# Storing the bias table of the sliding attention: one transfer in the second chunk of the projections, or sixteen in the seventh

## The chip, the cores and the metric

The kernel runs on one core of one Trainium2 chip. The metric is the device time of one execution in microseconds (us), as the median of the runs. The engines are named as in the profile: PE (TensorE, with PEld for its weight loads), DVE (VectorE), ACT (ScalarE), POOL (GpSimd) and SP (SyncE, which in this kernel issues nearly all DMAs). Each engine executes its instructions in the order in which they stand, and waits on semaphores for what others make.

## The reference, cut to what matters

The reference chains two transformer blocks over 2048 positions of width 1024. The first has a projection of 4096 columns, a differential and a dilated attention; the second is a sliding-window attention with sinks and a learned bias by distance.

```python
def first_block(x, p, mix_norm_g, w_in, ...):
    h = rms_norm(x, mix_norm_g[i])
    u = h @ w_in[i]                                   # (2048, 1024) @ (1024, 4096)
    dq, dk, dv, bq, bk, bv, z = jnp.split(u, IN_SPLIT_IDX, axis=-1)
    ...
    y = jnp.concatenate([a, b], axis=-1) * jax.nn.silu(z)

def banded_attention(q, k, v, t5_table, window, sinks=None):   # second block, window 128, 16 heads
    ...
    dist = nprev * Q_BLOCK + jnp.arange(Q_BLOCK)[:, None] - jnp.arange(kc)[None, :]
    valid = (dist >= 0) & (dist < window) & (kpos >= 0)
    bias = jnp.take(t5_table, t5_bucket(dist), axis=0)
    s = jnp.where(valid, s + bias[None, :, :, None], NEG)
    p = jax.nn.softmax(jnp.concatenate([s, sk], axis=-1), axis=-1)[..., :-1]
```

The bias of a head depends only on the distance between query and key. For 128 queries by 256 keys it is therefore a band matrix, every row of which is the row above, shifted by one.

## The kernel before, in words

The stages run one after the other: `phase_a` (the projection of the first block), `phase_b1` and `phase_b2` (its two attentions), `phase_c` (its output), `phase_d` (the sliding attention) and `phase_e` (the last product). A scheduler lays out the instructions of each engine while the program is built, by its own estimate of times and by the free buffers of the pools.

**phase_a** takes the 4096 columns in eight chunks of 512, in the order dv, bv, dk, dq, bk, bq, z0, z1 (`order`). A chunk is 16 tiles of 128 rows. A tile is 24 matmuls into one of four PSUM buffers `psm` (lines 190 to 192): eight pieces k of the depth, each with three products, since both operands are split in a high and a low part. After its last matmul a tile is evacuated by ACT and DVE into buffers of the pool `a_e` (14 buffers, printed as `t` or `t2`) and from there stored to DRAM: `evac_v` (lines 110 to 113, stores `s_dv` and `s_bv`), `norm_qk` and `trans_qk` (lines 128 to 161, stores such as `s_bq`), `evac_z` (lines 119 to 123, store `s_sz`).

The weights of the next chunk are loaded by `load_w` (lines 98 to 101): a DMA on SP into `wraw` (three buffers), a copy on ACT into the high part of `w`, a subtraction on POOL into the low part (ten buffers `w`). The ACT copies of the weights stand in the same queue as the evacuations of the tiles. With ten buffers `w`, two of the eight pieces of the next chunk can be converted while a chunk runs and three more wait in `wraw`; the other three are loaded as the chunk ends.

All these DMAs are issued by SP, in its order. The program gives them eight completion semaphores in turn, and a DMA waits for the one before it on its semaphore; so SP has at most eight DMAs open and stands still when the oldest of them isn't done.

**The bias table.** `prep_swa` is called (as `extra`) after the first chunk. One matmul (line 976) makes the 128 bias values of the 16 heads, DVE writes them into the middle of `e_vec`, 16 partitions (one for each head) of 384 numbers with -1e30 at both sides, and line 978 stores this row 128 times for every head into the DRAM table `s_toep` (16 x 128 x 384 numbers, 3,145,728 bytes):

```python
nc.sync.dma_start(scr["toep"], vec.unsqueeze(1).broadcast_to([16, P, 384]))
```

`phase_d` reads the table back with a row step of 383 instead of 384 numbers, which gives the shifted rows (`e_bias`, line 1092, first issued at 2159.2 us).

Of the kernel before, what the change touches and what calls it, by code (L numbers as in the profile page):

```python
# [7 lines left out]
F32 = mybir.dt.float32  # L8
# [8 lines left out]
P = 128  # L17
# [24 lines left out]
def phase_a(tc, c, x, w_in, mix_g, qk_gains, scr, extra):  # L42
    nc = tc.nc
    with (
# [19 lines left out]
        def tmp(dt=F32):  # L64
            return ep.tile([P, 512], dt, name="t2", tag="t2")
# [3 lines left out]
        def load_x(g, f):  # L69
            for j in range(4):  # L70
                t = tmp()
                nc.sync.dma_start(t, x[0, (4 * g + j) * P:(4 * g + j + 1) * P, 512 * f:512 * f + 512])
                xs[g, f, j] = t

        def trans_x(g, k):
            ps = pt.tile([P, 512], F32, name="pst")
            for j in range(4):
                nc.tensor.transpose(ps[:, j * P:(j + 1) * P], xs[g, k // 4, j][:, (k % 4) * P:(k % 4 + 1) * P], c["id"])
            nc.scalar.activation(hh[g][:, k], ps, AF.Copy, scale=g_t[:, k:k + 1])
            nc.vector.scalar_tensor_tensor(hl[g][:, k], ps, g_t[:, k:k + 1], hh[g][:, k].bitcast(F32),  # L80
                                           ALU.mult, ALU.subtract)
# [3 lines left out]
        def square_x(g, f):  # L85
            if f == 0:
                sq2s[g] = sp.tile([P, 2, 4], F32, name="sq2")
            for j in range(4):
                nc.scalar.activation(tmp(), xs.pop((g, f, j)), AF.Square, accum_out=sq2s[g][:, f, j:j + 1])
            if f == 1:  # L90
                ssq = sp.tile([P, 4], F32, name="ssq")
                nc.vector.tensor_add(ssq, sq2s[g][:, 0], sq2s[g][:, 1])
                rsqrt_dve(nc, sp, ssq, D, rstd[:, 4 * g:4 * g + 4])
                nc.vector.tensor_scalar(half_rstd[:, 4 * g:4 * g + 4], rstd[:, 4 * g:4 * g + 4], 0.5, None, ALU.mult)

        def load_w(ch, k):
            raw = wrp.tile([P, 512], F32, name="wraw")
            nc.sync.dma_start(raw, w_in[0, k * P:(k + 1) * P, ch * 512:(ch + 1) * 512])
            w = wp.tile([P, 2, 512], F32R, name="w")
            nc.scalar.activation(w[:, 0], raw, AF.Copy)  # L100
            nc.gpsimd.tensor_sub(w[:, 1], raw, w[:, 0].bitcast(F32))  # L101
            return w

        def evac_v(nm, t, ps):
            rs = rstd[:, t:t + 1]
            rows = slice(t * P, (t + 1) * P)
            w_ = 128 if nm == "dv" else 64
            ev = [tmp(F32R).rearrange("p (n w) -> p n w", w=w_) for _ in range(2)]
            psv = ps.rearrange("p (n w) -> p n w", w=w_)
            nc.scalar.activation(ev[0], psv, AF.Copy, scale=rs)  # L110
            nc.vector.scalar_tensor_tensor(ev[1], psv, rs, ev[0].bitcast(F32), ALU.mult, ALU.subtract)  # L111
            for i in range(2):
                nc.sync.dma_start(scr[nm][rows][:, :, i], ev[i].bitcast(F32))

        def evac_z(nm, t, ps):
            hr = half_rstd[:, t:t + 1]
            col = 512 * (nm == "z1")
            th = tmp()
            nc.scalar.activation(th, ps, AF.Tanh, scale=hr)
            nc.vector.tensor_scalar(th, th, 1.0, hr, ALU.add, ALU.mult)  # L120
            sz = tmp()
            nc.vector.tensor_tensor(sz, ps, th, ALU.mult)
            nc.sync.dma_start(scr["sz"][t * P:(t + 1) * P, col:col + 512], sz)
# [16 lines left out]
        def trans_qk(nm, t, qn):  # L140
            gain = gq[{"dq": 0, "dk": 1, "bq": 2, "bk": 3}[nm]]
            pq = pt.tile([P, 512], F32, name="pst")
            for f in range(4):
                nc.tensor.transpose(pq[:, f * P:(f + 1) * P], qn[:, f * P:(f + 1) * P], c["id"])
            th = tmp(F32R).rearrange("p (f t) -> p f t", f=4)
            tl = tmp(F32R).rearrange("p (f t) -> p f t", f=4)
            if nm == "bk":
                src, dh, dl = [w.rearrange("p (b u g) -> p g b u", u=16, g=4) if w is pq else
                               w.rearrange("p f (a g u) -> p g (f a) u", a=2, g=4) for w in (pq, th, tl)]
                nc.scalar.activation(dh.rearrange("p g b u -> p b u g"), src.rearrange("p g b u -> p b u g"),  # L150
                                     AF.Copy, scale=gain)
                for g in range(4):
                    nc.vector.scalar_tensor_tensor(dl[:, g], src[:, g], gain, dh[:, g].bitcast(F32),
                                                   ALU.mult, ALU.subtract)
            else:
                pq3 = pq.rearrange("p (f t) -> p f t", f=4)
                nc.scalar.activation(th, pq3, AF.Copy, scale=gain)
                nc.vector.scalar_tensor_tensor(tl, pq3, gain, th.bitcast(F32), ALU.mult, ALU.subtract)
            for i, src in ((0, th), (1, tl)):
                for e in range(2):  # L160
                    nc.sync.dma_start(scr[nm][:, e, i].rearrange("f d t -> d f t")[:, :, t * P:(t + 1) * P],
                                      src[64 * e:64 * e + 64].bitcast(F32))
# [13 lines left out]
        for i, ap in enumerate(qk_gains):  # L176
            t = cp.tile([P, 1], F32, name=f"qk_gain{i}")
            for half in range(2):
                nc.sync.dma_start(t[64 * half:64 * half + 64], ap.rearrange("o d -> d o"))
            gq.append(t)  # L180
        pend = []
        for oi, (nm, ch) in enumerate(order):
            nxt = []
            for t in range(NT):
                g, j = divmod(t, 4)
                ps = pm.tile([P, 512], F32, name="psm")
                for k in range(KD):
                    ah = hh[g][:, k, j * P:(j + 1) * P]
                    al = hl[g][:, k, j * P:(j + 1) * P]
                    nc.tensor.matmul(ps, ah, cur[k][:, 0], start=k == 0, stop=False)  # L190
                    nc.tensor.matmul(ps, al, cur[k][:, 0], start=False, stop=False)  # L191
                    nc.tensor.matmul(ps, ah, cur[k][:, 1], start=False, stop=k == KD - 1)  # L192
                if oi == 0 and g < 3:
                    if j == 0:
                        load_x(g + 1, 0)
                        load_x(g + 1, 1)
                    trans_x(g + 1, 2 * j)
                    trans_x(g + 1, 2 * j + 1)
                    if j == 3:
                        for f in range(2):  # L200
                            square_x(g + 1, f)
                if t >= 8 and oi + 1 < len(order):
                    nxt.append(load_w(order[oi + 1][1], t - 8))
                if len(pend) > 1 or pend and nm == "z0":
                    trans_qk(*pend.pop(0))
                if nm in ("dv", "bv"):
                    evac_v(nm, t, ps)
                elif nm in ("z0", "z1"):
                    evac_z(nm, t, ps)
                else:  # L210
                    pend.append((nm, t, norm_qk(nm, t, ps)))
            if oi == 0:
                extra(pt)
            cur = nxt
# [745 lines left out]
def prep_swa(tc, c, scr, table, onehot, sinks, pm):  # L960


    nc = tc.nc
    sk8 = c["const"].tile([P, 16], F32, name="e_sk")
    nc.sync.dma_start(sk8, sinks.broadcast_to([P, 16]))
    nc.vector.tensor_scalar(sk8, sk8, 8.0, None, ALU.mult)
    c["sk8"] = sk8
    with tc.tile_pool(name="p_c", bufs=1) as cp:
        tb = cp.tile([32, 16], F32, name="e_tb")
        nc.sync.dma_start(tb, table)  # L970
        oh = cp.tile([32, P], F32, name="e_oh")
        nc.sync.dma_start(oh, onehot)
        vec = cp.tile([16, 384], F32, name="e_vec")
        nc.vector.memset(vec, -1.0e30)
        ps = pm.tile([P, 512], F32, name="pst")[:16, :P]
        nc.tensor.matmul(ps, tb, oh, start=True, stop=True)
        nc.vector.tensor_scalar(vec[:, 128:256], ps, 8.0, None, ALU.mult)
        nc.sync.dma_start(scr["toep"], vec.unsqueeze(1).broadcast_to([16, P, 384]))


def phase_d(tc, c, scr, a_w_in):
# [393 lines left out]
```

## Time and profile before

| | us |
|---|---|
| median of 3 runs | 2957.75 (2957.2 to 2959.73) |
| the profiled execution | 2958.66 |
| its span, first to last instruction | 2956.9 |
| PE busy in the span | 2878.8 (97%) |
| bias table: store issued | 114.0 |
| bias table: first read issued | 2159.2 |

The profiled execution lies 0.91 us above the median and its span 1.76 us below its own time. A row of a timeline gives the start, the length, engine, line and operation, the tiles, and in brackets the idle time of the engine just before with what ended it. A window row gives for a stretch the busy time of each engine with the count of instructions, then the granted clock of TensorE (1.00 is the higher level, 2.4 GHz, 0.50 the lower, 1.2 GHz), the mean busy share of the 16 DMA engines, and the GB/s that they moved. A row of the DMA issues gives the KB of one transfer and the us from issue to landing.

### The profile page before, as it was taken

What the parts mean: (1) busy time and instruction counts of PE and PEld (TensorE: products, weight loads), DVE (VectorE), ACT (ScalarE), POOL (GpSimd) and SP (SyncE); (2) the same over time, 40 slices, a digit from 0 to 9 for tenths busy, and PEclk for the clock granted to TensorE, in tenths of its full rate; (3) what the DMA queues carried; (4) which work ended last, traced back from release to release, by engine and by line L of the source; (5) the groups of instructions that cost most, each with busy time, mean ns of one, the idle gap of its engine ahead of it and who ended that gap; (6) DMA issues with size and microseconds to landing.
All of it is one profiled execution on the core that took longest, in us unless ns stands there. A gap on an engine that the chain in (4) does not pass through costs nothing.

```text
span 2956.9 us, 45164 instructions
## 1 busy us (share of the span) xinstructions
PE 2878.8 (97%) x15554; PEld 2455.2 (83%) x15554; DVE 1803.7 (61%) x4607; ACT 1562.5 (53%) x3480; POOL 1239.1 (42%) x1156
## 2 busy tenths in 40 slices
PE   9999999999999999989999899999999999999998
PEld 7878888888798888878999778888788888888787
DVE  4215556522688888887877654444535756666855
ACT  5222333221588888878989442222345756665621
POOL 1110111001488888864777700000156555555421
PEclk9999999999999999999999899999999999999999
DMA  6663444424314132129786633232554243332552
GB/s 208 116 160 86 122 114 121 96 87 115 121 30 115 46 106 65 51 64 189 143 164 133 180 116 110 77 113 92 183 166 155 86 157 96 109 100 72 156 182 79
DMA packets 410646, 346.00 MB, mean 117 GB/s; under 512 B 89745, under 2 KB 356401, under 8 KB 408497
## 3 DMA queue, kind: packets, MB, share of 16 engines
q1 hardware_dynamic: 388000, 329.24, 40.2%
q10 hardware_dynamic: 20736, 8.65, 1.8%
q0 software_dynamic: 1680, 5.21, 0.7%
q8 instruction: 124, 2.03, 0.3%
q14 instruction: 106, 0.86, 0.1%
HBM read 227.51 MB, written 116.52 MB: 116 GB/s over the span
## 4 chain that ended last, share of the span: by engine, by line
PE 86%; DMA 5%; DVE 3%; ACT 2%; SPq 1%; issue 1%; POOL 0%; DVEq 0%; ACTq 0%; POOLq 0%
PE s_ps L331 8%; PE psm L190 7%; PE psm L192 7%; PE psm L191 7%; PE e_mm L804 5%; PE e_mm L806 5%; PE e_mm L805 5%; PE c_mm L804 4%; PE c_mm L805 4%; PE c_mm L806 4%; PE t_ps L375 3%; PE o_ps L389 2%; PE o_ps L391 2%; PE o_ps L390 2%; PE d_sr L590 2%; PE f_mm L805 2%
## 5 line engine op out<-in xcount | busy, mean ns | idle before, releaser
L190 PE MATMUL psm<-w,hh 128*128 128x512 f32 x1024 | 406.3, 398 | 9.4 <-DVE t L111 8.0
L191 PE MATMUL psm<-w,hl 128*128 128x512 f32 x1024 | 399.5, 391 | 0.0
L192 PE MATMUL psm<-w,hh 128*128 128x512 f32 x1024 | 399.5, 393 | 0.0
L101 POOL TENSOR_TENSOR w<-wraw,w 128x512 fp32r<-128x512 f32 x64 | 81.5, 1294 | 600.2 <-ACT w L100 589.9
L365 POOL TENSOR_TENSOR et<-et 128x1024 f32<-128x1024 f32 x124 | 296.0, 2409 | 0.0
L331 PE MATMUL s_ps<-kst,qst 128*128 128x512 f32 x1024 | 289.7, 407 | 5.5 <-DVE mx L337 3.7
L347 ACT ACTIVATE et<-et,nm 128x2048 f32<-128x2048 f32 x128 | 257.2, 2009 | 5.2
L1026 POOL TENSOR_TENSOR e_wt<-e_raw,e_wt 128x1024 fp32r<-128x1024 f32 x80 | 191.3, 2399 | 111.9 <-ACT e_wt L1025 110.9
L190 PEld LDWEIGHTS psm<-w,hh 128*128 128x128 f32 x1024 | 193.5, 189 | 48.3 <-DVE t L111 8.4
L804 PE MATMUL e_mm<-e_x,e_wt 128*128 128x512 f32 x576 | 228.2, 396 | 1.2 <-DVE e_k L1068 0.8
L806 PE MATMUL e_mm<-e_x,e_wt 128*128 128x512 f32 x576 | 226.8, 394 | 0.0
L192 PEld LDWEIGHTS psm<-w,hh 128*128 128x128 f32 x1024 | 192.9, 189 | 40.9
L805 PE MATMUL e_mm<-e_x,e_wt 128*128 128x512 f32 x576 | 226.6, 393 | 0.0
L191 PEld LDWEIGHTS psm<-w,hl 128*128 128x128 f32 x1024 | 193.7, 189 | 38.2
L331 PEld LDWEIGHTS s_ps<-kst,qst 128*128 128x128 f32 x1024 | 175.9, 190 | 45.3 <-DVE mx L337 18.1
L1127 POOL TENSOR_SCALAR e_es<-e_es,e_l 128x256 f32<-128x256 f32 (+1 forms) x256 | 119.4, 485 | 170.8 <-DVE e_l L1125 118.6
L364 POOL TENSOR_SCALAR et<-et,cc 128x1024 f32<-128x1024 f32 x124 | 138.2, 1129 | 110.3 <-PE psm L192 57.1
L377 DVE TENSOR_TENSOR ptl<-t_ps,pth 128x512 fp32r<-128x512 f32 x256 | 169.4, 684 | 19.9 <-ACT pth L376 16.8
L337 DVE CUSTOM_DVE_ANT_0 et<-s_ps,nd,mx 128x1024 f32<-128x1024 f32 x128 | 163.9, 1280 | 26.5 <-PE s_ps L331 24.7
L1114 DVE CUSTOM_DVE_ANT_0 e_es<-e_s,e_bias,e_sk 128x256 f32<-128x256 f32 (+1 forms) x256 | 117.4, 473 | 102.6 <-PE e_s L1106 71.2
L376 ACT ACTIVATE pth<-t_ps 128x512 fp32r<-128x512 f32 x256 | 143.6, 595 | 44.8 <-PE t_ps L375 41.1
L850 POOL TENSOR_TENSOR c_yn<-c_yn,ssq_sub 128x512 f32<-128x512 f32 x16 | 17.0, 1061 | 354.1 <-DMA c_yn<-s_y 354.1
(268 smaller groups left out, 7848.2 us busy)
## 6 DMA issues: line engine op xcount, KB each, us to landing
e_raw<-in_a_w_in_dram SPq DMA_DIRECT2D x80, 512.0 KB, 3.7
wraw<-in_w_in_dram SPq DMA_DIRECT2D x64, 256.0 KB, 3.5
kst<-s_dk SPq DMA_DIRECT2D x128, 128.0 KB, 4.2
s_xt<-c_at SPq DMA_DIRECT2D x32, 512.0 KB, 6.8
e_x<-s_xt SPq DMA_DIRECT2D x32, 512.0 KB, 7.1
t<-in_x_dram SPq DMA_DIRECT2D x32, 256.0 KB, 5.4
s_dv<-t SPq DMA_DIRECT2D x32, 256.0 KB, 3.3
s_bv<-t SPq DMA_DIRECT2D x32, 256.0 KB, 3.6
```

Source lines behind the costliest of these rows:

```text
L190: nc.tensor.matmul(ps, ah, cur[k][:, 0], start=k == 0, stop=False)
L191: nc.tensor.matmul(ps, al, cur[k][:, 0], start=False, stop=False)
L192: nc.tensor.matmul(ps, ah, cur[k][:, 1], start=False, stop=k == KD - 1)
L331: nc.tensor.matmul(ps[:, b * 512:b * 512 + 512], lhs, heads[h, "k", e, i, 2 * hf + b], start=i == 0, stop=i == 1)
L337: nc.vector.tensor_tensor_reduce(et[:, hf], ps, bias[:, off:off + 1024], 1.0, -3.0e38 if hf == 0 else mx[:, 0:1], ALU.add, ALU.max, mx[:, ...
L347: nc.scalar.activation(ev, ev, AF.Exp, bias=nm, scale=slope, accum_out=st[g]["l"][:, e:e + 1])
L365: nc.gpsimd.tensor_sub(es[0][:, hf], es[0][:, hf], es[1][:, hf])
L377: nc.vector.tensor_sub(tl[:, :, qi], pt, th[:, :, qi].bitcast(F32))
L804: nc.tensor.matmul(ps, ah, bh, start=first, stop=False)
L805: nc.tensor.matmul(ps, al, bh, start=False, stop=False)
L806: nc.tensor.matmul(ps, ah, bl, start=False, stop=last)
L1026: nc.gpsimd.tensor_sub(w[:, 1], raw, w[:, 0].bitcast(F32))
```

## The change

The store of the table is taken out of `prep_swa`. The pool of `e_vec` becomes `a_c`, which lives as long as `phase_a`, and in the seventh chunk (z0) each of the 16 tiles issues the store of one head, 128 x 384 numbers or 196,608 bytes, from the one partition of `e_vec` that holds the head. `keep_in_program_order` marks each of these DMAs for the scheduler. In the built program the heads go out in the order 8, 9, 0, 10, 11, 1, 2, 12, 3 to 7, 13, 14, 15, and the first read of the table stands behind all of them.

```diff
+        c["a_c"] = cp
         pend = []
         for oi, (nm, ch) in enumerate(order):
             nxt = []
@@
                     nxt.append(load_w(order[oi + 1][1], t - 8))
                 if len(pend) > 1 or pend and nm == "z0":
                     trans_qk(*pend.pop(0))
+                if nm == "z0":
+                    tc.keep_in_program_order(nc.sync.dma_start(
+                        scr["toep"][t], c["vec"][t:t + 1].unsqueeze(1).broadcast_to([1, P, 384])))
                 if nm in ("dv", "bv"):
@@ prep_swa
-        vec = cp.tile([16, 384], F32, name="e_vec")
+        vec = c["a_c"].tile([16, 384], F32, name="e_vec")
         nc.vector.memset(vec, -1.0e30)
         ps = pm.tile([P, 512], F32, name="pst")[:16, :P]
         nc.tensor.matmul(ps, tb, oh, start=True, stop=True)
         nc.vector.tensor_scalar(vec[:, 128:256], ps, 8.0, None, ALU.mult)
-        nc.sync.dma_start(scr["toep"], vec.unsqueeze(1).broadcast_to([16, P, 384]))
+    c["vec"] = vec
```

In the built program PE, ACT and POOL keep their order. On DVE the fill of `e_vec` (line 974) moves some thirty rows forward, and SP's order changes at three places. Lines below 181 keep their number; of the later ones, `s_sz` stays line 123, `wraw` line 98, and the new store is line 208.

The first place is SP's queue at the end of the first chunk, before:

```order
L113 DMA s_dv_90<-t2_1169 512x1x128
L98 DMA wraw_1127<-in_w_in_dram 128x512
L98 DMA wraw_1163<-in_w_in_dram 128x512
L98 DMA wraw_1199<-in_w_in_dram 128x512
L978 DMA s_toep_136<-e_vec_1238 2048x1x384
L113 DMA s_dv_90<-t2_1204 512x1x128
L98 DMA wraw_1518<-in_w_in_dram 128x512
L113 DMA s_dv_90<-t2_1205 512x1x128
L98 DMA wraw_1554<-in_w_in_dram 128x512
```

and now:

```order
L113 DMA s_dv_90<-t2_1169 512x1x128
L98 DMA wraw_1127<-in_w_in_dram 128x512
L98 DMA wraw_1163<-in_w_in_dram 128x512
L98 DMA wraw_1199<-in_w_in_dram 128x512
L113 DMA s_dv_90<-t2_1204 512x1x128
L98 DMA wraw_1517<-in_w_in_dram 128x512
L113 DMA s_dv_90<-t2_1205 512x1x128
L98 DMA wraw_1553<-in_w_in_dram 128x512
```

The store of the table is gone from between the weights of the second chunk (`wraw_1127` to `wraw_1199`, its pieces 5 to 7) and those of the third (`wraw_1518` onward).

The second place is SP's queue where z0 begins. The `wraw` rows are pieces 0 to 4 of z1's weights, the `s_bq` rows the last tiles of the sixth chunk. Before:

```order
L161 DMA s_bq_88<-t2_5427 64x4x128 x2
L98 DMA wraw_5750<-in_w_in_dram 128x512
L98 DMA wraw_5786<-in_w_in_dram 128x512
L98 DMA wraw_5822<-in_w_in_dram 128x512
L161 DMA s_bq_88<-t2_5481 64x4x128 x2
L161 DMA s_bq_88<-t2_5482 64x4x128 x2
L98 DMA wraw_5858<-in_w_in_dram 128x512
L98 DMA wraw_5894<-in_w_in_dram 128x512
L123 DMA s_sz_137<-t2_5492 128x512
```

and now:

```order
L161 DMA s_bq_88<-t2_5426 64x4x128 x2
L98 DMA wraw_5757<-in_w_in_dram 128x512
L208 DMA s_toep_136<-e_vec_1238 128x1x384
L98 DMA wraw_5794<-in_w_in_dram 128x512
L208 DMA s_toep_136<-e_vec_1238 128x1x384
L161 DMA s_bq_88<-t2_5480 64x4x128 x2
L161 DMA s_bq_88<-t2_5481 64x4x128 x2
L208 DMA s_toep_136<-e_vec_1238 128x1x384
L98 DMA wraw_5831<-in_w_in_dram 128x512
L208 DMA s_toep_136<-e_vec_1238 128x1x384
L123 DMA s_sz_137<-t2_5492 128x512
L98 DMA wraw_5868<-in_w_in_dram 128x512
```

Stores of the table now stand between the weight loads, and the stores `s_sz` of the first tiles follow behind them. Up to the store of tile 7, thirteen heads have been issued in all; then eight `s_sz` follow with none between.

The third place is SP's queue at the end of z0, where the `wraw` rows are pieces 5 to 7 of z1's weights. Before:

```order
L123 DMA s_sz_137<-t2_5974 128x512
L98 DMA wraw_5930<-in_w_in_dram 128x512
L98 DMA wraw_5966<-in_w_in_dram 128x512
L98 DMA wraw_6002<-in_w_in_dram 128x512
L123 DMA s_sz_137<-t2_6010 128x512
```

and now:

```order
L123 DMA s_sz_137<-t2_5988 128x512
L98 DMA wraw_5942<-in_w_in_dram 128x512
L208 DMA s_toep_136<-e_vec_1238 128x1x384
L98 DMA wraw_5979<-in_w_in_dram 128x512
L208 DMA s_toep_136<-e_vec_1238 128x1x384
L98 DMA wraw_6016<-in_w_in_dram 128x512
L208 DMA s_toep_136<-e_vec_1238 128x1x384
L123 DMA s_sz_137<-t2_6025 128x512
```

The last three heads stand between and behind the last three weight loads; fifteen of the sixteen are ahead of the last load, `wraw_6016`.

## Rows read from the trace of the kernel before

**Rows 1.** The page: busy time of TensorE, and the transfer of the table.

```profile
PE 2878.8 (97%) x15554; PEld 2455.2 (83%) x15554; DVE 1803.7 (61%) x4607; ACT 1562.5 (53%) x3480; POOL 1239.1 (42%) x1156
...
s_toep<-e_vec SPq DMA_DIRECT2D x1, 3072.0 KB, 35.5
```

**Rows 2.** Windows of 40 us about the end of the first chunk.

```profile
80.00:120.00 40.00, 40.00 (x186) 32.88 (x185) 10.55 (x28) 14.77 (x32) 7.60 (x6) 1.00 0.43 110
120.00:160.00 40.00, 31.97 (x131) 25.91 (x130) 4.23 (x6) 4.95 (x8) 2.53 (x2) 0.88 0.95 152
```

**Rows 3.** Timeline of SP's queue, 105 to 175 us.

```profile
114.01 0.65 SPq L978 DMA_DIRECT2D s_toep<-e_vec  x1
115.16 10.16 SPq L113 DMA_DIRECT2D s_dv<-t  x1
125.42 7.70 SPq L98 DMA_DIRECT2D wraw<-in_w_in_dram  x1
133.21 4.52 SPq L113 DMA_DIRECT2D s_dv<-t  x1
137.84 9.05 SPq L98 DMA_DIRECT2D wraw<-in_w_in_dram  x2
```

**Rows 4.** Timeline of ACT, 95 to 240 us.

```profile
150.98 0.63 ACT L100 ACTIVATE w<-wraw 128x512 fp32r<-128x512 f32 x1 [25.48 <-DMA wraw<-in_w_in_dram]
...
153.05 2.40 ACT L110 ACTIVATE t<-psm,rstd_x 128x512 fp32r<-128x512 f32 x4
```

**Rows 5.** The waits of the stretch 90 to 260 us: TensorE's own.

```profile
PE psm L190 <- DVE t L111: 8.0, 1, 8.0
```

**Rows 6.** The critical chain about 154 to 162 us: start, length of the step, what.

```profile
154.56 0.80 PE psm L190
...
156.21 0.43 PE psm L190
...
160.05 0.40 PE psm L190
...
160.93 0.23 PE psm L190
```

**Rows 7.** DMA queue of SP, 116 to 145 us: packets, MB, share of 16 engines.

```profile
q1 hardware_dynamic: 1860, 2.85, 91.5%
```

**Rows 8.** The same queue, 612 to 668 us, and its transfers.

```profile
q1 hardware_dynamic: 1440, 2.62, 12.1%
...
s_sz<-t SPq DMA_DIRECT2D x10, 256.0 KB, 2.0
```

**Rows 9.** The same queue, 520 to 580 us, and its transfers.

```profile
q1 hardware_dynamic: 10884, 5.25, 37.4%
...
s_bq<-t SPq DMA_DIRECT2D x42, 128.0 KB, 2.5
```

**Rows 10.** Windows of 10 us in z0.

```profile
590.00:600.00 10.00, 10.00 (x48) 8.24 (x47) 5.31 (x12) 5.79 (x10) 5.09 (x4) 1.00 0.82 223
...
640.00:650.00 10.00, 10.00 (x46) 8.29 (x45) 2.36 (x4) 1.20 (x2) 0.00 (x0) 1.00 0.14 52
```

**Rows 11.** Timeline of SP's queue, 585 to 700 us.

```profile
591.43 2.59 SPq L161 DMA_DIRECT2D s_bq<-t  x4
594.11 1.52 SPq L98 DMA_DIRECT2D wraw<-in_w_in_dram  x3
...
675.23 2.82 SPq L98 DMA_DIRECT2D wraw<-in_w_in_dram  x3
```

**Rows 12.** Tile wraw, 585 to 690 us: from issue to landing.

```profile
DMA to landing us min/median/max: 2.7/3.1/4.1
```

**Rows 13.** Timelines of ACT and POOL where z1 begins.

```profile
680.59 0.63 ACT L100 ACTIVATE w<-wraw 128x512 fp32r<-128x512 f32 x1 [0.30 <-DMA wraw<-in_w_in_dram]
686.51 0.69 ACT L119 ACTIVATE t<-psm,half_rstd 128x512 f32<-128x512 f32 x1 [5.29 <-PE psm L192]
...
679.00 3.98 POOL L101 TENSOR_TENSOR w<-wraw,w 128x512 fp32r<-128x512 f32 x3 [1.30 <-ACT w L100]
```

## The prediction, made before the changed kernel was run

> **What bounds the kernel now.** I read the page first: TensorE is busy for 97% of the span [rows 1], so an edit off TensorE can only win where TensorE stands idle or slow, and lose where it makes new idle time. Windows over the projection show one such place: from 120 to 160 us TensorE is busy for 31.97 of 40 us at a mean clock of 0.88, while the 16 DMA engines are 95% busy; the window ahead has neither [rows 2]. SP's timeline shows why the DMA engines are full: the store of the table is issued at 114.01, and the four rows behind it take 10.16, 7.70, 4.52 and 9.05 us to issue, where such a row otherwise takes well under one [rows 3, 11]. The table's store takes 35.5 us to land [rows 1], and what is issued later lands later.
>
> The victim is a weight load that nobody needs yet. Line 98 at 125.42 loads the first piece of the third chunk's weights, wanted a whole chunk later; but its copy on ACT (line 100) stands ahead of the evacuations. ACT waits 25.48 us for it, then evacuates four tiles in a row (line 110, x4) [rows 4]. With all four PSUM buffers full, TensorE waits 8.0 us for the evacuation [rows 5]. Then it runs at the lower clock: the chain goes from 154.56 to 160.45 in 13 steps, most of 0.43 us, where later steps take 0.23 [rows 6]. That is 5.89 us for work of 13 x 0.227 = 2.95 us, a loss of 2.9. The store costs **8.0 + 2.9 = 10.9 us** where it stands.
>
> **The change, part by part.**
>
> *Removed: the store in the second chunk.* Nothing else in SP's order there changes, so the weights follow at once, ACT doesn't wait, and the 10.9 us are won in full: the chunk's DMAs alone are covered, as they are in the window before the store (DMA share 0.43, TensorE without idle time [rows 2]).
>
> *Moved: the fill of `e_vec`* (one DVE operation) comes earlier in DVE's queue, and `e_vec` keeps its own room; DVE is busy 10.55 of 40 us there [rows 2]. Cost nothing, and at most its own fraction of a microsecond if DVE were the bound.
>
> *Added: sixteen stores on SP in z0.* z0 looks like a good place: at 640 to 650 us the DMA engines are 14% busy [rows 10]. What counts is how long one store holds the rings, which the trace doesn't show for a source of one partition. The nearest rows:
>
> - The old store, from 16 partitions: 2.85 MB in 29 us, or 98 GB/s, with the rings busy all the time [rows 7].
> - The store `s_sz`, from 128 partitions: 2.62 MB in 12.1% of 56 us, or 387 GB/s [rows 8].
>
> If a head keeps the old pace, it takes a sixteenth of the old store: 196,608 bytes / 98 GB/s = 2.0 us. If the pace falls with the count of partitions, 98/16 = 6.1 GB/s give 32 us. I take a value between, since the rows fit a step: 98 and 387 are 4 and 16 times 24.2 to 24.5 GB/s. With such units one partition has at least one, 24.4 GB/s, and 196,608 / 24.4 = **8.06 us** for one head. That is nearest to what both rows show together, and it says that sixteen DMA engines queue for one unit.
>
> The Trainium skill has the unit as a rule, in "SBUF — State Buffer", section "Door 1: The DMA port swizzle": a transfer is as fast as the number of 16 SBUF ports that its partitions reach; partitions 0 to 15 reach four (104 GB/s measured there), partitions 0 to 3 one (27.6 GB/s). The 98 GB/s of this trace agree with the four. By its 27.2 GB/s for a port a head would take 7.2 us, an estimate, and the sum below would be 15 x 0.86 = 13 us smaller.
>
> Now the queue. The rings serve SP's DMAs in the order of issue, as the 25 us wait for the weights showed. Fifteen heads stand ahead of the last weight load of z1 (the third place in the order), so that load comes no earlier than their sum:
>
> - Start: z1's first load is at 594.11 before [rows 11], so the first head is issued at 594.5 - 10.9 = 583.6. Four `s_bq` and one load are ahead of it; the head starts at about 585.1.
> - 15 heads x 8.06 = 120.9 us.
> - Between them: 7 weight loads and 15 `s_sz` of 262,144 bytes at 387 GB/s, 22 x 0.68 = 15.0 us; 8 `s_bq` of 131,072 bytes, 8 x 0.56 = 4.5 us (5.25 MB in 37.4% of 60 us are 234 GB/s [rows 9]). Together 19.5 us.
> - The load ends at 585.1 + 120.9 + 19.5 = 725.5. The shortest landing is 2.7 us [rows 12], of which 0.7 is the transfer: +2.0. Then the copy (0.63) and the subtraction (3.98/3 = 1.3) [rows 13]: 729.4.
> - From there tile 0 of z1 still has its last six matmuls in TensorE's queue, some of tile 1 among them: 1.4 us, end at 730.8. Before, its evacuation began at 686.5, released by TensorE [rows 13]. The difference is **+44.3 us**, with the 10.9 of the first place already in it.
>
> Two corrections. The 19.5 us of other transfers need other partitions, and a ring that is through with its share of a head can go on; between nothing and all of it is hidden, and I take half: -9.8. And after the last stall TensorE restarts at the lower clock, as it did at 154.56: +2.9 (at the stalls before it, the DMA sets the pace and this costs nothing). Sum: 44.3 - 9.8 + 2.9 = **+37.4 us**. On the way TensorE also stalls inside z0: the `s_sz` stores are stuck behind heads and hold their buffers `t2`, of which there are 14 and a tile takes two; those stalls lie within the 44.3, since the last load ends the wait anyhow.
>
> Against the profiled execution: 2958.66 + 37.4 = 2996.1, which stands 0.9 us above the median of the runs; **2996 us**. The ends of this case: all of the other transfers hidden and no lower clock, 44.3 - 19.5 = +24.8, 2983; nothing hidden and the lower clock twice, +50, 3009.
>
> **The rivals.**
>
> *The sixteen stores are hidden; the kernel gets faster.* The old row bounds a head at 2.0 us if the 98 GB/s are a limit of the engines' own (each re-reading one row) and not of the source. Then 16 x 2.0 = 32 us fit into z0 (594 to 681 us [rows 11, 13]) with the rings 14% busy [rows 10]. Only the load behind two heads at the third place comes up to 4.0 us later. Its subtraction ends at 683.0 before, 3.5 us ahead of the evacuation at 686.5 [rows 13], of which the six matmuls take 1.4; so at most 4.0 - 2.1 = 1.9 us are lost there, and the rest of the 10.9 is won: 2948 to 2950. Against it: the two rates stand at exactly 4 to 16. The point that decides is the time of one head. Each microsecond of it is worth 15 us, so the +37.4 vanish at 8.06 - 37.4/15 = 5.6 us.
>
> *One partition gives less than a unit.* At half a unit a head takes 16 us and the sum grows by 15 x 8.06 = 121 to about 3117; at 6.1 GB/s it goes beyond 3300. No row shows a unit divided; the trace has no store from fewer than 16 partitions with any weight.
>
> *In between.* Heads of 4 to 6.4 us, because the sixteen rings overlap better than a queue, leave 2949 to 2971, around no change.
>
> *The removal doesn't help.* The third chunk's first load could still hold ACT up, since its copy still stands ahead of the evacuations; then +10.9 more. Against it: without the store the queue ahead of that load is two ordinary transfers.
>
> **How the numbers follow.** Forecast 0.68; hidden 0.19; in between 0.08; less than a unit 0.05 (the removal that doesn't help is a small part of the forecast's upper end). What a measurement of this kernel tells from no change is about 0.2%, or 6 us: faster, 0.19 + 0.03 of the in-between = 0.22; same 0.03; slower 0.68 + 0.02 + 0.05 = 0.75. The range must take in the hidden case, or more than 2 in 10 would be left out: 2946 to 3010. It leaves out the case of less than a unit. The forecast's own range is 2983 to 3009.
>
> **What the changed profile would show.** Step one is right if TensorE has no idle time between 120 and 160 us and the waits of line 111 there are gone. The unit is right if the new stores take 8 us of ring time each, so that the DMA engines are near 100% busy at some 25 GB/s through z0, and if ACT's copy of line 100 or the evacuations of z0 and z1 wait long for DMAs. The queue is right if TensorE's idle time lies at the end of z0 and the start of z1, up to about 730 us, and sums to 45 to 50 us. The prediction is wrong at its root if a head lands in 3 to 4 us and z0 stays at full pace; it is wrong in the queue if heads are slow but loads issued behind them land in their 3 us.

## The result, and the profile after

The changed kernel takes **2978.65 us** (median of 4 runs, 2978.13 to 2983.99), the kernel before 2958.74 us (4 runs, 2957.2 to 2962.71). The ratio is **1.0069**, 95% interval [1.0052, 1.0087]: slower by about 20 us. The forecast was slower, at 2996 us: the sign is right, the time lies inside the stated range of 2946 to 3010 us, and the size is 17 us too large. It lies 4 us below the 2983 to 3009 us that the forecast's own mechanism was given. The profiled run is the slowest of its four (2983.99 us, span 2982.2); a second profile of the same kernel (below) has a span of 2978.8.

**The gain at the old place came in full.** The two windows that answer to [rows 2] (bounds, time and TensorE's busy time, then PEld, DVE, ACT, POOL, granted clock, DMA share, GB/s):

```profile
80.00:120.00 40.00, 40.00 (x186) 32.87 (x185) 10.89 (x28) 15.33 (x34) 7.59 (x6) 1.00 0.40 121
120.00:160.00 40.00, 40.00 (x178) 33.14 (x177) 6.01 (x8) 6.54 (x10) 2.58 (x2) 1.00 0.44 118
```

From 120 to 160 us TensorE is busy for all 40 us at the full clock, where [rows 2] had 31.97 at 0.88. The wait of [rows 5] is gone. z1's first weight load is issued at 583.49 us, against 594.11 in [rows 11]: 10.6 of the 10.9 us that were forecast are there at the start of z0.

**The loss is where it was looked for.** Windows from z0 to the first tiles of z1:

```profile
600.00:650.00 50.00, 50.00 (x222) 41.44 (x221) 9.89 (x18) 6.30 (x10) 0.00 (x0) 1.00 0.85 77
650.00:720.00 70.00, 47.20 (x160) 35.64 (x159) 11.72 (x19) 8.48 (x13) 7.76 (x6) 0.80 0.76 88
```

In [rows 10] the DMA engines were 14% busy at 640 to 650 us. Now they are 85% busy from 600 to 650, and they move only 77 GB/s. TensorE holds out on its buffers until 650; from there to 720 it is busy for 47.20 of 70 us at a mean clock of 0.80.

What stalls there, as the waits of 560 to 760 us have it (engine, tile and line, what it waited for: total us, times, longest):

```profile
DVE t L122 <- DMA s_sz<-t: 46.5, 5, 13.2
ACT w L100 <- DMA wraw<-in_w_in_dram: 45.1, 7, 17.7
```

Both are waits for transfers that only share the rings (SP's queue over the 16 DMA engines) with the table: the stores of z0's results, which give back the buffers that DVE writes, and the weight loads of z1. SP's timeline of the last heads, and ACT's at the same time, show the order in which they come (start, us, what; in brackets the idle time before and its releaser):

```profile
686.49 0.59 SPq L98 DMA_DIRECT2D wraw<-in_w_in_dram  x1
687.13 0.65 SPq L208 DMA_DIRECT2D s_toep<-e_vec  x1
687.87 0.54 SPq L98 DMA_DIRECT2D wraw<-in_w_in_dram  x1
688.46 4.73 SPq L208 DMA_DIRECT2D s_toep<-e_vec  x1
693.28 0.54 SPq L98 DMA_DIRECT2D wraw<-in_w_in_dram  x1
```

```profile
690.33 0.63 ACT L100 ACTIVATE w<-wraw 128x512 fp32r<-128x512 f32 x1 [17.66 <-DMA wraw<-in_w_in_dram]
...
697.97 0.63 ACT L100 ACTIVATE w<-wraw 128x512 fp32r<-128x512 f32 x1 [6.43 <-DMA wraw<-in_w_in_dram]
705.33 0.63 ACT L100 ACTIVATE w<-wraw 128x512 fp32r<-128x512 f32 x1 [6.73 <-DMA wraw<-in_w_in_dram]
708.98 0.69 ACT L119 ACTIVATE t<-psm,half_rstd 128x512 f32<-128x512 f32 x1 [3.02 <-PE psm L193]
712.25 0.69 ACT L119 ACTIVATE t<-psm,half_rstd 128x512 f32<-128x512 f32 x1 [2.59 <-PE psm L193]
```

Between two of these loads in the queue stands one head. The copies are 7.64 and 7.36 us apart; less the 0.68 us of the load itself, a head holds the rings for 7.0 and 6.7 us, **6.8 us** in round numbers, or 196,608 bytes / 6.8 us = 28.9 GB/s. That is the number on which the case turns. The first evacuation of z1 begins at 708.98, against 686.51 in [rows 13]: 22.5 us later. The second begins at 712.25, 23.5 us later than before:

```profile
688.78 0.69 ACT L119 ACTIVATE t<-psm,half_rstd 128x512 f32<-128x512 f32 x1 [1.58 <-PE psm L192]
```

Most of that is still there when the bias table is first read (20.9 us) and at the end (25.3 us).

The DMA view of 640 to 690 us shows the pace directly (40 slices of 1.25 us; busy tenths, then GB/s moved):

```profile
DMA  9878998575988989989965879787997892999999
GB/s 33 35 30 77 194 34 25 21 177 95 29 27 26 28 39 168 70 26 29 29 57 184 34 25 33 23 29 143 107 30 25 26 30 54 386 380 379 377 299 86
```

While only a head moves, the engines are mostly 70 to 99% busy and deliver 21 to 39 GB/s. The peaks between are single `s_sz` stores and loads. When eight `s_sz` come in a row (the last slices), the same engines move 380 GB/s at the same busy share.

### The profile page after: what moved, and what is told of

Read it like the earlier page. It is cut to its first block, busy times and chain, and to the rows that moved or that the text cites. A ratio compares the mean times of both kernels' runs of the same rounds, so it can differ in the third digit from the quotient of the medians.

```text
span 2982.2 us, 45182 instructions
## 1 busy us (share of the span) xinstructions
PE 2890.1 (97%) x15554; PEld 2460.6 (83%) x15554; DVE 1806.5 (61%) x4607; ACT 1562.2 (52%) x3480; POOL 1239.8 (42%) x1156
## 5 line engine op out<-in xcount | busy, mean ns | idle before, releaser
L191 PE MATMUL psm<-w,hh 128*128 128x512 f32 x1024 | 408.7, 401 | 24.9 <-ACT w L100 12.7
```

## The experiments

Each is compared with runs of the kernel before on the same chip; the ratios are of those, with 95% intervals. The expectations in us are meant for the chip of the result above, where the kernel before takes 2959 us; elsewhere it takes up to 2965, so an expectation is to be compared with the ratio and not with the measured us. The diffs are against the changed kernel. Every kernel stores the whole table.

### The changed kernel once more

> The changed kernel once more, for a second profile of it on the chip of the other runs: 2976 to 2984 us, last weight load of z1 landing near 705 us, TensorE idle about 28 us between 650 and 710 us.

Measured: 2978.39 us, ratio 1.0070 [1.0052, 1.0088]; TensorE busy for 45.33 of the 70 us from 650. The first evacuation of z1 begins at 708.74, 22.2 us later than before, and this run ends 21.9 us above the profiled run of before. So the shift at z1 repeats within 0.3 us, and the 3 us between the two profiles of this kernel arise in later stages, which the change doesn't touch.

### Sixteen partitions for each store, at the same sixteen places

```
-   scr["toep"][t], c["vec"][t:t + 1].unsqueeze(1).broadcast_to([1, P, 384])
+   scr["toep"][:, 8 * t:8 * t + 8], c["vec"].unsqueeze(1).broadcast_to([16, 8, 384])
```

> Sixteen stores of 196,608 bytes at the sixteen places of the changed kernel, but each takes 8 rows of all 16 heads, so its source is 16 partitions instead of one. Theory (a store from one partition is slow, 6.8 us of ring time by the spacing of the last weight loads of the changed kernel, 7.64 and 7.36 us less 0.68): a store now takes 196,608 / 98 GB/s = 2.0 us, nothing waits in z0, and only the 10.9 us of the first place remain as a gain: 2948 us. Rival (sixteen issues among the weight loads are the cost, whatever they read): about 2979 us, as the changed kernel.

Measured: 2944.3 us, ratio **0.9956** [0.9941, 0.9971]. The place, the count of stores, the bytes of each and the queue are as in the changed kernel; only the source is now all 16 partitions, each giving 8 rows. The window of 650 to 720 us and the issue rows of the table's stores (duration of the SP row in ns min/median/max; us of the first and the last; they land 3.5/5.1/6.2 us after their issue, min/median/max):

```profile
650.00:720.00 70.00, 70.00 (x310) 58.01 (x309) 16.16 (x27) 12.65 (x19) 8.42 (x7) 1.00 0.39 110
```

```profile
L208 SPq DMA_DIRECT2D s_toep<-e_vec x16: 431/1322/1522, 583.6 to 667.3; - x16
```

TensorE has no idle time left there, and the whole 10.9 us of the first place is won: 0.44% of 2959 us is 13 us, [9, 17] by the interval. The issue rows of the changed kernel, whose stores land after 8.9/13.1/17.2 us:

```profile
L208 SPq DMA_DIRECT2D s_toep<-e_vec x16: 558/3878/7922, 584.1 to 693.9; - x16
```

So the loss is due to the form of the stores, not to moving them, splitting them or putting them into z0.

### Four partitions: neighbours, and four apart

Both stores take 4 heads x 32 rows, so they agree in bytes, rows and number of partitions. The first takes the heads of four neighbouring partitions, the second every fourth.

```
-   scr["toep"][t], c["vec"][t:t + 1].unsqueeze(1).broadcast_to([1, P, 384])
+   hs, rs = slice(t // 4 * 4, t // 4 * 4 + 4), slice(t % 4 * 32, t % 4 * 32 + 32)
+   scr["toep"][hs, rs], c["vec"][hs].unsqueeze(1).broadcast_to([4, 32, 384])
```

```
-   scr["toep"][t], c["vec"][t:t + 1].unsqueeze(1).broadcast_to([1, P, 384])
+   hs, rs = slice(t // 4, 16, 4), slice(t % 4 * 32, t % 4 * 32 + 32)
+   scr["toep"][hs, rs], c["vec"][hs].unsqueeze(1).broadcast_to([4, 32, 384])
```

> As the changed kernel, but each store takes 32 rows of four neighbouring heads (partitions 0 to 3, 4 to 7 and so on). Theory of the unit (neighbours share one unit): 6.8 us for each store as before, 2976 to 2982 us. Rival (the limit is that of a single partition): four partitions give four times the pace, 1.7 us, nothing waits, 2948 us. The Trainium skill, SBUF - State Buffer, section Door 1, puts partitions 0 to 3 on one port, which would be the first.

> As the run with neighbouring heads, with the same bytes, rows and number of partitions, but the four heads of a store are four partitions apart (0, 4, 8, 12 and so on). Theory of the unit: four units instead of one, 196,608 / 98 GB/s = 2.0 us, 2948 us. Rival (single partitions): as fast as neighbours, so both runs alike, 2948 us. Rival (four DMA engines only, since the first dimension is four): both alike and slow.

Measured: neighbours 2991.4 us, ratio **1.0117** [1.0098, 1.0136]; four apart 2946.49 us, ratio **0.9960** [0.9945, 0.9976]. The DMA views, of 650 to 700 us for the neighbours (in the midst of their backlog) and of 600 to 650 us for four apart (where eight of its stores stand; the slices are 1.25 us again):

```profile
DMA  3222234222342222252222262262262265765662
GB/s 99 41 24 23 23 82 124 87 36 23 75 131 29 38 38 33 48 159 25 38 38 36 27 182 23 32 194 33 36 181 27 30 222 221 288 251 234 210 196 57
```

```profile
DMA  6872263545226322521022000500050002300050
GB/s 186 219 277 103 110 245 145 216 164 195 97 101 257 116 99 86 212 100 55 0 113 97 0 0 0 210 0 0 0 210 0 0 0 90 120 0 13 0 216 0
```

And the two windows of 650 to 720 us, neighbours first:

```profile
650.00:720.00 70.00, 38.14 (x120) 28.29 (x119) 8.07 (x14) 7.11 (x11) 7.62 (x6) 0.79 0.34 81
```

```profile
650.00:720.00 70.00, 70.00 (x311) 57.95 (x310) 16.15 (x27) 12.65 (x19) 8.41 (x7) 1.00 0.36 110
```

The neighbours fall to 23 to 38 GB/s while a store of theirs moves, the rate of a single partition, although they are four. Four apart show 86 to 120 GB/s in twelve of their slices and more in others; from 600 to 620 us, where eight of the sixteen stores are issued, no slice falls below 86. So what has a rate of its own is not a partition but a group of partitions: partitions 0 to 3 share one unit, and 0, 4, 8 and 12 lie in four. This is the rule of the Trainium skill ("SBUF — State Buffer", section "Door 1: The DMA port swizzle"), in which the two lowest bits of the partition's number don't choose the port; the pair of runs bears it out. The two runs also differ in where they write: the blocks of one store lie 196,608 bytes apart in DRAM for neighbours and 786,432 for four apart. The rows of eight above write blocks 196,608 bytes apart as well and are fast, so that distance isn't the cause.

The neighbours show one thing more. While they move, the DMA engines are mostly just 20 to 40% busy (a quarter would be four of the sixteen, one for each partition; that is a guess, as the view doesn't show single engines), and yet they cost more than single heads with a busy share of 85%. The busy share tells nothing of how long the queue is held.

### Single heads at the old place

The sixteen stores stand where the kernel before has its one store.

```
-                if nm == "z0":
-                    tc.keep_in_program_order(nc.sync.dma_start(
-                        scr["toep"][t], c["vec"][t:t + 1].unsqueeze(1).broadcast_to([1, P, 384])))
...
+        for t in range(16):
+            nc.sync.dma_start(scr["toep"][t], vec[t:t + 1].unsqueeze(1).broadcast_to([1, P, 384]))
```

> The sixteen stores of one head each, all at the old place in the second chunk; nothing of the table in z0. Theory (6.8 us for a head, served in order): the rings are held 16 x 6.8 = 109 us instead of 35.5, so the stall there grows by about 73 us: 2958.7 + 73 = 3032 us. Rival (the number of bytes sets the time, and the place z0 is what costs): the same stall as the old store, 2959 us.

Measured: 3038.69 us against 2965.48, ratio 1.0245 [1.0221, 1.0269], **+73 us**. The SP queue and ACT's wait, from the timeline of 100 to 210 us and the waits of 90 to 260 us:

```profile
117.59 0.57 SPq L980 DMA_DIRECT2D s_toep<-e_vec  x1
123.65 88.31 SPq L980 DMA_DIRECT2D s_toep<-e_vec  x15
```

```profile
ACT w L100 <- DMA wraw<-in_w_in_dram: 101.9, 4, 97.6
...
PE psm L191 <- DVE t L111: 79.6, 1, 79.6
```

Sixteen heads in a row give the cost of a head without other transfers between: the middle issue row takes 6.84 us (574/6838/7324 ns). The wait for the weights is 97.6 us where the one store had 25.48 [rows 4], and TensorE waits 79.6 us where it had 8.0 [rows 5]: 71.6 us more. The remainder of the 73 is within the error of the comparison.

### One whole store in z0

```
-                if nm == "z0":
+                if nm == "z0" and t == 4:
...
-                        scr["toep"][t], c["vec"][t:t + 1].unsqueeze(1).broadcast_to([1, P, 384])))
+                        scr["toep"], c["vec"].unsqueeze(1).broadcast_to([16, P, 384])))
```

> The old store in one piece from 16 partitions, issued at the fifth tile of z0. Theory: the rings are held 32 us, from about 615 to 647 us; no weight load is wanted there and ACT has none in its queue, and the stores s_sz that wait hold at most 6 x 2 of the 14 buffers: 2948 us. Rival (any 35 us of held rings stall TensorE in z0 as they did in the second chunk): 2955 to 2959 us.

Measured: 2954.25 us against 2965.48, ratio 0.9963 [0.9949, 0.9977]. The old store, with its landing of 35.5 us as in [rows 1], costs nothing when it is issued at 604.3 us, behind z1's first five weight loads and 60 us ahead of its last three (664.57). TensorE is busy for all of 600 to 720 us at clock 1.00. Moving the table is worth 11 us; the split into sixteen isn't needed for it.

### Fewer heads in z0: one per two tiles over two chunks, and three of them in z1

```
-                if nm == "z0":
+                if nm in ("bq", "z0") and t % 2:
+                    hd = t // 2 + 8 * (nm == "z0")
...
-                        scr["toep"][t], c["vec"][t:t + 1].unsqueeze(1).broadcast_to([1, P, 384])))
+                        scr["toep"][hd], c["vec"][hd:hd + 1].unsqueeze(1).broadcast_to([1, P, 384])))
```

```
-                if nm == "z0":
+                if nm == "z0" and t < 13 or nm == "z1" and 3 <= t < 6:
+                    hd = t if nm == "z0" else t + 10
...
-                        scr["toep"][t], c["vec"][t:t + 1].unsqueeze(1).broadcast_to([1, P, 384])))
+                        scr["toep"][hd], c["vec"][hd:hd + 1].unsqueeze(1).broadcast_to([1, P, 384])))
```

> The sixteen stores of one head each, from one partition, but one in two tiles, over the sixth and seventh chunk (bq and z0). Theory: a head is still 6.8 us of ring time, but two tiles give 10.9 us and the other transfers need 2 x 0.7 in z0 and about 4.5 in bq, so the queue never grows for long: 2948 to 2952 us. Rival (stores from one partition among the loads cost by themselves): 2975 us or more.

> As the changed kernel, but the last three heads are issued at tiles 3 to 5 of z1, behind its weight loads; thirteen remain in z0. Theory (a queue, in which the last load waits for every head ahead of it): two heads fewer ahead of the last load, 2 x 6.8 = 13.6 us less: 2979 - 13.6 = 2965 us. Rival (the stall is set by the buffers of the evacuations inside z0, not by the last loads): 2975 us or more.

Measured: spread 2966.34 us against 2965.48, ratio 1.0003 [0.999, 1.0016]; last three later 2974.86, ratio 1.0027 [1.0013, 1.0041].

The second came as expected: of the fifteen heads ahead of z1's last load thirteen are left, and the two fewer are worth 12.5 us by the ratios (1.0069 to 1.0027 of 2965 us; their intervals allow some 7 us either way), where 13.6 had been put down. The first missed: 2948 to 2952 of 2959 us are ratios of 0.9964 to 0.9977, so it is 8 to 12 us above them. The rows say why. The seven heads of bq that the timeline shows between 500 and 592 us, and the next weight load:

```profile
507.12 0.62 SPq L209 DMA_DIRECT2D s_toep<-e_vec  x1
519.84 0.62 SPq L209 DMA_DIRECT2D s_toep<-e_vec  x1
...
581.03 0.62 SPq L209 DMA_DIRECT2D s_toep<-e_vec  x1
589.80 0.55 SPq L98 DMA_DIRECT2D wraw<-in_w_in_dram  x1
```

```profile
593.82 0.63 ACT L100 ACTIVATE w<-wraw 128x512 fp32r<-128x512 f32 x1 [12.28 <-DMA wraw<-in_w_in_dram]
...
607.99 0.64 ACT L100 ACTIVATE w<-wraw 128x512 fp32r<-128x512 f32 x1 [10.20 <-DMA wraw<-in_w_in_dram]
```

bq is busy with stores of its own: 6.8 us of head and eight `s_bq` of 0.56 us are 11.3 us, two tiles of bq last 11.8 us (evacuations 5.91 us apart), and the heads follow each other every 12.0 to 12.7 us. That leaves no slack: z0's last weight loads are issued at 589.80, where the changed kernel issues them at 576.08, and ACT waits 12.28 and 10.20 us for weights. TensorE is busy for 13.39 of the 20 us from 580 and for 16.93 of the 20 us from 680. The loss is smaller than the changed kernel's, but two thirds of TensorE's idle time (6.6 of 9.7 us) have moved to the start of z0.

### One head per two tiles over z0 and z1

```
-                if nm == "z0":
+                if nm in ("z0", "z1") and t % 2:
+                    hd = t // 2 + 8 * (nm == "z1")
...
-                        scr["toep"][t], c["vec"][t:t + 1].unsqueeze(1).broadcast_to([1, P, 384])))
+                        scr["toep"][hd], c["vec"][hd:hd + 1].unsqueeze(1).broadcast_to([1, P, 384])))
```

> Edit: the sixteen stores of one head each stay, but one is issued at every other tile of z0 and z1, not at every tile of z0. Theory (a head occupies the rings for 6.8 us, and what stalls the engines is the backlog): two tiles of this stretch last about 10.9 us, and 6.8 us of head with about 1.4 us of the stretch's other transfers fit in, so no backlog builds up; TensorE has no idle stretch between 650 and 720 us, and the stall of the changed kernel is gone with the first store's 10.9 us still won: about 2948 us, ratio 0.996 to 0.998; a head that lands late in z1 may cost the start of the next stage up to 8 us (2956, ratio 1.000). Rival (every store from one partition stalls the stretch by itself, whatever its spacing): the time of the changed kernel, ratio 1.005 or above, with ScalarE waiting for wraw at the start of z1.

Measured: 2971.64 us against 2965.05, ratio 1.0022 [1.0012, 1.0031]: above the first expectation and below the rival's. Windows of TensorE, this kernel and the kernel before:

```profile
600.00:660.00 60.00, 60.00 (x267) 49.69 (x266) 12.96 (x22) 7.59 (x11) 0.00 (x0) 1.00 0.63 89
660.00:680.00 20.00, 16.95 (x68) 13.57 (x67) 2.91 (x4) 5.04 (x8) 7.61 (x6) 0.89 0.67 73
720.00:760.00 40.00, 33.69 (x129) 25.68 (x128) 9.21 (x16) 5.75 (x8) 0.00 (x0) 0.88 0.76 150
760.00:800.00 40.00, 32.61 (x127) 24.47 (x126) 21.08 (x35) 15.28 (x22) 9.99 (x7) 0.84 0.76 168
```

```profile
660.00:680.00 20.00, 20.00 (x90) 16.55 (x89) 4.01 (x7) 5.52 (x9) 4.80 (x4) 1.00 0.23 79
720.00:760.00 40.00, 40.00 (x179) 33.10 (x178) 13.56 (x24) 9.43 (x13) 2.24 (x2) 1.00 0.57 171
760.00:800.00 40.00, 34.66 (x163) 25.94 (x162) 28.68 (x52) 22.78 (x33) 19.90 (x14) 0.96 0.45 138
```

z0 runs through to 660 us without a stall, so spacing does end the backlog there. Then two heads are issued close together among z1's weight loads (at 665.15 and 671.02), and TensorE loses 3.05 us. From 720 to 800 us it loses 6.3 and 2.1 us more: z1 is the stretch in which the next stage loads its `kst`, and the heads stand ahead of those loads; SP's longest row for one grows from 1.09 to 7.18 us. The lost time, 11.4 us of TensorE and something for the clock at 0.84 to 0.89, is more than the 10.9 that the first place gave back. So the rival's mechanism (stall whatever the spacing) is out, and so is the expectation that spacing alone is enough: a head delays whatever urgent load stands behind it, in z1 as in z0.

### The heads on another queue

```
-   tc.keep_in_program_order(nc.sync.dma_start(
+   tc.keep_in_program_order(nc.gpsimd.dma_start(
```

> The sixteen stores of one head each at the places of the changed kernel in the code, but issued by POOL on its own queue, so SP's loads and stores don't stand behind them in a ring. Theory of order (what stands behind a head in the same ring waits for it): loads and s_sz land nearly as before, 2948 to 2955 us. Rival (a DMA engine that is busy with a head is slow for every queue): 2970 us or more, with long landings on SP's queue too.

Measured: 3003.74 us against 2964.25, ratio **1.0136** [1.0119, 1.0153]. ACT's longest wait of 560 to 760 us and TensorE's worst window:

```profile
ACT t L119 <- DMA s_bq<-t: 43.5, 1, 43.5
```

```profile
620.00:640.00 20.00, 6.39 (x29) 4.96 (x27) 0.00 (x0) 0.00 (x0) 0.00 (x0) 0.79 0.89 41
```

POOL issues eight heads in one row of 4.36 us at 587.39, and stores of `s_bq` that SP issues from 587.86 on hold ACT up for 43.5 us. A queue of their own doesn't free the others from the heads: the DMA engines are 89% busy at 41 GB/s. The Trainium skill has this as a rule ("DMA: Bandwidth & Descriptors", section "Issuing engines are not separate DMA queues"): DMAs run on the same 16 DMA engines and interleave there, whichever engine started them. This trace agrees, at the price of another 20 us over the changed kernel (1.0136 - 1.0069 = 0.0067 of 2964). What makes up these 20 us isn't separated: besides the other queue, eight heads go out at once here, and POOL's own work on the weights (line 101) stands behind heads that wait 5.0 and 11.1 us for earlier ones.

### Sixteen partitions, in the second chunk

```
-                if nm == "z0":
+                if nm == "bv":
...
-                        scr["toep"][t], c["vec"][t:t + 1].unsqueeze(1).broadcast_to([1, P, 384])))
+                        scr["toep"][:, 8 * t:8 * t + 8], c["vec"].unsqueeze(1).broadcast_to([16, 8, 384])))
```

> Edit: the table is stored in sixteen pieces of eight rows of all sixteen heads, as in the run with rows of eight, but at the sixteen tiles of the second chunk (bv), where the kernel before has its one store, not of z0. Theory (form decides, not place): a piece from sixteen partitions occupies the rings for about 2.0 us and sixteen of them 32 us over a stretch of some 88 us, so the stall of 8.0 us before the third chunk is gone as it was in z0: about 2948 us, ratio 0.995 to 0.997. Rival (place decides: this stretch already moves the second chunk's weights and inputs, and has no room for the table in any form): the stall stays where it is, 2958 us, ratio 0.999 to 1.001.

Measured: 2957.74 us against 2965.05, ratio 0.9967 [0.9955, 0.9978]. The window that [rows 2] has for before:

```profile
120.00:160.00 40.00, 40.00 (x178) 33.15 (x177) 5.25 (x7) 5.99 (x9) 3.79 (x3) 1.00 0.97 191
```

TensorE is busy for all 40 us with the DMA engines 97% busy, more than the 95% of before. The same stretch, as full of transfers as it was, has room for the table if it comes in sixteen pieces, about 2 us each by the 98 GB/s of [rows 7], and not in one of 32. The place, then, is worth little: 0.9956 in z0 and 0.9967 here can't be told apart by their intervals.

## Why the prediction came out as it did

**Removal: right.** 10.9 us were forecast for the first place. The window there is full at clock 1.00, and the four kernels that free it without a new stall (rows of eight in z0 and in bv, four apart, the whole store in z0) gain 0.33 to 0.44%, 10 to 13 us.

**The unit: right in kind, mis-sized.** The step "98 and 387 are 4 and 16 times 24.2 to 24.5 GB/s" was read as the rate of one unit, and a head came to 8.06 us. It takes 6.8 us, 28.9 GB/s. Fifteen heads make 15 x 1.26 = **18.9 us** of it, the largest single error. The step that failed is the division: a sixteenth of what 16 units deliver together was taken for what one delivers alone. Eight `s_sz` in a row still move 380 GB/s in the trace of after, 16 x 23.8, while one unit alone reaches 28.9; a unit alone is a fifth faster than its share of all. The prediction also took the rings to be busy all the time in [rows 7], which has 91.5%; that isn't a gap that explains the difference, since heads in a row at the old place show 84% (130 to 205 us) with the next head always waiting in the queue. The Trainium skill's 27.2 GB/s for a port ("SBUF — State Buffer", section "Door 1: The DMA port swizzle") gave an estimate of 7.2 us and a sum smaller by 13 us, +24, next to the 23.5 seen; the head itself is a little faster than that. That the two sums meet is luck in part: 0.4 us too much for each of fifteen heads, 6 us, goes against an overlap that was put 6.5 us too high.

**The queue in order: right.** With 6.8 us the same sum gives 585.1 + 15 x 6.8 + 19.5 + 2.0 = 708.6 us for the last load; ACT takes it at 705.3.

**The overlap: too large.** Half of the other transfers' 19.5 us were to lie beside the heads. From 708.6 and 705.3 it is about 3 us, a sixth. That is an inference from the sum, not a measurement of its own: with 6.7 or 7.0 us for a head it is 2 or 6 us. It is below half either way, and the DMA view agrees with that, in which the `s_sz` peaks of 143 to 194 GB/s stand as slices of their own between the heads. The error of 9.8 - 3.3 = 6.5 us goes against that of the unit: -18.9 + 6.5 = -12.4, and the load came 717.7 - 705.3 = 12.4 us before its forecast.

**The clock: right; the step before it: too long.** TensorE after the last stall:

```profile
706.01 0.80 PE L191 MATMUL psm<-w,hh 128*128 128x512 f32 x1 [4.43 <-ACT w L100]
...
707.88 1.05 PE L193 MATMUL psm<-w,hh 128*128 128x512 f32 x2
...
711.59 0.40 PE L192 MATMUL psm<-w,hl 128*128 128x512 f32 x1
```

Thirteen steps take 5.58 us, most of them 0.43, where 13 x 0.227 = 2.95 would do: 2.6 us lost, for 2.9 in the sum (2.3 in the second profile). But TensorE begins at 706.01, 0.68 us after ACT's copy begins. The sum let it wait for the copy and the subtraction, 1.93 us; the trace has the products with the high part (lines 191 and 192) first and those with the low part (line 193) behind, so POOL's subtraction runs beside them. That saves 1.25 us.

**Together.** 37.4 - 12.4 for the load, - 1.25 for the subtraction and - 0.3 for the clock give 23.5, which is the shift seen at z1. The medians are 20 us apart; the remaining 3 us lie in later stages, where two profiles of the changed kernel differ by as much.

**The idle time: half of what was to be seen.** The prediction looked for 45 to 50 us of idle TensorE up to 730 us; it waits 22.8 us, up to 706. The stall in z0 and z1 costs 22.5 us at the first evacuation and the 10.9 us gained before, 33.4 in all. TensorE stands still for 22.8 of them; the other 10.6 fit the time that it works at the lower clock between the waits (mean 0.80 from 650 to 720 us). As the sum says, only what lies behind the last load counts.

**The rivals.** "Hidden" fell at its own point of decision: a head takes 6.8 us, more than the 5.6 us from which the sum turns. By the measured terms that point lies lower still: each microsecond of head is worth 15 us, so a gain would have needed about 6.8 - 23.5/15 = 5.2 us. The rival was the right mechanism for the wrong form, since the run with rows of eight from 16 partitions has about its time: 0.9956 of before, or 2946, for 2948 to 2950. "Less than a unit" is out, as a head takes 6.8 us and not 16 or more. "The removal doesn't help" is out by the window at 120 us. The `t2` buffers were named as a stall inside z0 that the last load covers; they took 10.4 of the 22.8 us that TensorE waited from 560 to 760 (12.4 at ACT's copies), and the end was set by the last load.

## What to carry to other kernels

A store that broadcasts from few partitions is better cut so that each piece still reads from several units (all 16 partitions, or four that are four apart) than by single partitions: sixteen pieces of the same bytes cost nothing with all 16 partitions in each and 20 us with one in each. Before a transfer is moved to a quiet stretch, ask how long it holds the queue for each of the loads that stand behind it, and compare that with the slack of the most urgent one; the busy share of the DMA engines answers neither, and neither the two spacings tried here, nor another queue, nor a later chunk for some of them made up for a piece that is too slow. And the rate of one source alone is not the rate of many divided by their count: it has to be measured alone.

## What was unexpected of the hardware

- Four neighbouring partitions are no faster than one (23 to 38 GB/s while they move) and stall the kernel more (1.0117 against 1.0069), with the DMA engines only 20 to 40% busy. ACT takes z1's last load at 715.40 there, 10.1 us after the changed kernel, so each of the fifteen stores ahead takes 0.7 us more. Why isn't settled: their bytes are the same.
- The DMA engines can be 97% busy for 40 us without TensorE losing anything (sixteen pieces in the second chunk, 191 GB/s), and 14 us of idle time can arise in 20 us at 89% (heads on POOL's queue, 41 GB/s).
- Heads on POOL's queue hold up SP's stores so long that ACT waits 43.5 us at a stretch; its longest wait for a transfer in the changed kernel is 17.7 us.
